# Expert weights loaded as rows of 8 KB per partition, gate and up accumulated over the full hidden width

## The chip, the core and the metric

The kernel runs on one core of one Trainium2 chip. Its engines are TensorE (PE, with PEld for the loading of the stationary operand), VectorE (DVE), ScalarE (ACT), GpSimd (POOL) and SyncE (SP); SP issues most of the DMAs, which 16 DMA engines carry out. The metric is the device time of one execution in microseconds.

## The reference, cut to what matters

One layer of a diffusion backbone over 512 latent tokens of width 1024. The part that the change touches is the last one, a mixture of 16 experts in which every expert picks its 64 best tokens:

```
D_MODEL = 1024; SEQ = 512; N_EXPERTS = 16; EC_CAPACITY = 2; D_EXPERT = 2048

def ec_moe(h, w_router, w_gate, w_up, w_down):
    b, l, d = h.shape
    cap = EC_CAPACITY * l // N_EXPERTS                      # 64 tokens for each expert
    aff = jax.nn.softmax((h @ w_router).astype(jnp.float32), axis=-1)
    gates, idx = lax.top_k(jnp.swapaxes(aff, 1, 2), cap)
    xs = jax.vmap(lambda hb, ib: hb[ib])(h, idx)
    hid = jax.nn.silu(jnp.einsum('becd,edf->becf', xs, w_gate)) * jnp.einsum('becd,edf->becf', xs, w_up)
    ys = jnp.einsum('becf,efd->becd', hid, w_down) * gates[..., None].astype(h.dtype)
    return jax.vmap(lambda yb, ib: jnp.zeros((l, d), yb.dtype).at[ib.reshape(-1)].add(yb.reshape(-1, d)))(ys, idx)
```

Ahead of it stand the adaLN modulation, a state-space branch, a differential attention and their merge; behind it a normalisation and the residual. All is float32. Each expert has three matrices of 8 MiB (gate and up 1024 x 2048, down 2048 x 1024), 24 MiB in all, 384 MiB for the 16 experts.

## The kernel before, in words

The program is written for one core with its order written out by hand: each engine runs its instructions in program order, and every load of an expert's weights is issued on SP in the order in which the code comes to it.

**Weight tiles.** `load_w` (L1579) takes the next free slot from the queue `E` and loads 1 MiB into it, 128 partitions x 2048 floats. A slot is one of the rotating buffers (tile name `we`), one of three pieces of a larger buffer (`wl`), or once each the buffers `gm` and `mo` before their later use. `done_w` puts the slot back in the queue behind the matmuls that read it. SP waits there until PE has released the slot, and then issues the next load. The load (L1592) takes two blocks of 128 rows, each 1024 floats (4 KB) wide: `"(k p) f -> p k f"`, so partition p gets row p and row 128 + p of the tile.

**One expert.** `hidden(e)` (L1629) works on half of the hidden width at a time (b = 0, 1). For each half it goes through four tiles of gate and then four of up, and accumulates both over the 1024 input channels in two PSUM tiles of tag `gu` (four buffers). A tile feeds two steps of 128 channels, each with two matmuls of 512 columns: the 64 tokens are the stationary operand, and the two matmuls write the lower and the upper 64 partitions of the accumulator. Each matmul shows as two records in the trace, so a tile is 8 records at L1643. Then ACT forms the Silu of gate into `sgm` (L1650), DVE multiplies by up (L1651), PE transposes the four blocks of 128 columns (L1654) into a PSUM tile `ht`, and DVE copies them to `hid` (L1655), from which `expert(e)` (L1657) takes the stationary operands of the down matmuls. Down has eight tiles of 256 rows (L1670), again two steps of 128 channels with two matmuls.

**Pairs.** Experts are gathered and scattered in pairs. After the hidden part of an odd expert, and ahead of its down, `gather` selects the tokens of the next pair with matmuls against a one-hot matrix (L1612), which DVE prepares (L1604). After an even expert `spread` (L1624) transposes the pair's gate-weighted one-hot matrix; after an odd one `scatter` adds the pair's output to the accumulators `facc` (L1684 to L1689). The first pair's gather is a generator, `first`, of which `hidden(0)` takes two steps ahead of each of its first tiles.

**The last expert.** After `hidden(15)` the down matrix is read in column blocks of 512, 256 and 256, with rows of 2 KB and 1 KB, in eight loads, and the closing normalisation of the first blocks runs between them. The output is stored at L1762.

**An earlier weight load with other rows.** The modulation weights (tile `araw`, L1099) are loaded as `w_ada[128 * (n % 8):128 * (n % 8) + 128, c0:c0 + 2048]`, 128 partitions with 8 KB each. The residual input (tile `x`, L1382) is loaded in eight parts of 32 partitions with 8 KB each.

Of the kernel before, what the change touches and what calls it, by code (L numbers as in the profile page):

```python
# [12 lines left out]
AF = mybir.ActivationFunctionType  # L13
OP = mybir.AluOpType
# [3 lines left out]
D = 1024  # L18
# [7 lines left out]
NE = 16  # L26
CAP = 64
FF = 2048
# [5 lines left out]
def layer(ctx: ExitStack, tc: tile.TileContext, A, out):  # L34
    nc = tc.nc
    PE, V, S, GP, DMA = nc.tensor, nc.vector, nc.scalar, nc.gpsimd, nc.sync
# [48 lines left out]
    def bank(name="b"):  # L85
        turn_[0] += 1
        if three[0] and turn_[0] % 3 == 0:
            return cbank(name)
        if three[0] is None:
            return pb.tile([128, 512], F32, name=name, tag="b")  # L90
        pair_[0] += 1
        return pb.tile([128, 512], F32, name=name, tag="bd"[pair_[0] % 2])
# [82 lines left out]
    ident = keep.tile([128, 128], F32, name="ident")  # L175
# [371 lines left out]
    for q in range(4):  # L547
        for par in range(2):
            PE.matmul(tl[64 * par:64 * par + 64, 64 * q:64 * q + 64], L[:, q], ident[0:64, 0:64],
                      start=True, stop=True, skip_group_check=True)  # L550
# [176 lines left out]
    for s in range(1, 96):  # L727
# [4 lines left out]
        sq = keep.tile([128, 2, 2, 16], F32, name="sq", bufs=2)  # L732
# [8 lines left out]
    def cobank(name):  # L741
# [8 lines left out]
                     op=OP.mult)  # L750
# [41 lines left out]
    wv = []  # L792
# [147 lines left out]
    for f in range(2):  # L940
        pgs = [bank2("glu")[:, 0:512] for _ in range(2)]
        for kt in range(4):
            for m in range(2):
                for n, (a, b) in enumerate(PASSES):
                    PE.matmul(pgs[m], wg[a][:, 512 * kt + 256 * f + 128 * m:512 * kt + 256 * f + 128 * m + 128], ygp[b][kt],
                              start=kt == 0 and n == 0, stop=kt == 3 and n == 2)
# [15 lines left out]
    for n in range(8):  # L962
        pq = bank("proj")
# [73 lines left out]
    for p in range(4):  # L1037
        t, w = kw.pop(0)
# [283 lines left out]
    pq = {}  # L1322
# [30 lines left out]
    for n in range(8, 16):  # L1353
        m = n % 8
# [33 lines left out]
    def psum(name, tag):  # L1388
        return ps_.tile([128, 512], F32, name=name, tag=tag, bufs=dict(s=2, gu=4, t=1, y=1)[tag])

    u_ = Carve(big("U2", "mo"))
    yp_, oh, sgm = u_(128, 2, D), u_(128, 4, 2, CAP), u_(128, 512)
# [175 lines left out]
    xst = [t[:, D:2 * D].rearrange("p (d e s) -> p d e s", d=8, e=2) for t in (gf_, gm_)]  # L1568
    hid = []
    wl = big("SR", "wl")  # L1570

    def strs(n):

        tags = [x for x in E if isinstance(x, str)][-n:]
        for x in tags:
            E.remove(x)
        return tags

    def load_w(src, r0, c0, cols=1024, n=1):  # L1579

        tag = E.popleft()
        if isinstance(tag, str):
            wv = regs.tile([128, 2048], F32, name="we", tag=tag)
        elif tag[0] == "SR":
            wv = wl[:, 2048 * tag[1]:2048 * tag[1] + 2048]
        else:
            wv = gm_ if tag[0] == "gm" else yp_.rearrange("p b d -> p (b d)")
        k = 2048 // cols
        wv = wv.rearrange("p (k f) -> p k f", k=k)
        for i in range(n):  # L1590
            a, b = k // n * i, k // n * (i + 1)
            DMA.dma_start(out=wv[:, a:b], in_=src[r0 + 128 * a:r0 + 128 * b, c0:c0 + cols].rearrange("(k p) f -> p k f", p=128))  # L1592
        return wv, tag

    def done_w(tag):
        if tag[0] not in ("U2", "gm"):
            E.append(tag)
# [8 lines left out]
    def gather(ep):  # L1606

        pick(ep, lambda i, n: r2[:, i:i + 1])
        for d in range(8):
            pg = psum("gat", "sst"[d % 3] if ep == 0 else "s")[:, 0:128]  # L1610
            for i in range(4):
                PE.matmul(pg, x1[i][:, 128 * d:128 * d + 128], oh[:, i].rearrange("p e s -> p (e s)"), start=i == 0, stop=i == 3)  # L1612
            o = xst[ep % 2][:, d].rearrange("p e s -> p (e s)")
            if d % 2:
                S.activation(o, pg, AF.Identity, scale=fs[:, 1, d:d + 1], bias=fs[:, 0, d:d + 1])
            else:
                V.tensor_scalar(o, pg, fs[:, 1, d:d + 1], fs[:, 0, d:d + 1], op0=OP.mult, op1=OP.add)
            yield
# [8 lines left out]
    wgt, wup, wdn = A["w_exp_gate"][0], A["w_exp_up"][0], A["w_exp_down"][0]  # L1627

    def hidden(e):  # L1629
        if not hid:  # L1630
            hid.append(None)
        for b in range(2):
            pgu = []
            for src in (wgt, wup):
                pq = psum("gu", "gu")
                for hk in range(4):
                    for _ in range(2):
                        next(first, None)
                    wv, tag = load_w(src[e], 256 * hk, 1024 * b)
                    for k in range(2):  # L1640
                        kt = 2 * hk + k
                        for j in range(2):
                            PE.matmul(pq[64 * j:64 * j + 64], xst[e // 2 % 2][:, kt, e % 2],  # L1643
                                      wv[:, k, 512 * j:512 * j + 512], start=kt == 0, stop=kt == 7, skip_group_check=True)
                    done_w(tag)
                pgu.append(pq)
            if hid[0] is None:
                t = regs.tile([128, 2048], F32, name="hid", tag=strs(1)[0])
                hid[0] = t.rearrange("p (b f i m) -> p b f i m", b=2, f=2, i=4)
            S.activation(sgm, pgu[0], AF.Silu)  # L1650
            V.tensor_tensor(sgm, sgm, pgu[1], op=OP.mult)  # L1651
            pt = psum("ht", "t")
            for i in range(4):
                PE.transpose(pt[:, 128 * i:128 * i + 128], sgm[:, 128 * i:128 * i + 128], ident)  # L1654
            V.tensor_copy(hid[0][:, e % 2, b].rearrange("p i m -> p (i m)"), pt)  # L1655

    def expert(e):  # L1657
        hidden(e)
        if e % 2:
            for _ in gather(e // 2 + 1):  # L1660
                pass
        hT_ = hid[0][:, e % 2]
        py = psum("yd", "y")
        for q in range(8):
            wv, tag = load_w(wdn[e], 256 * q, 0)
            b, jf = q // 4, (q % 4) // 2
            for k in range(2):
                i = 2 * (q % 2) + k
                for j in range(2):
                    PE.matmul(py[64 * j:64 * j + 64], hT_[:, b, i, 64 * jf:64 * jf + 64],  # L1670
                              wv[:, k, 512 * j:512 * j + 512], start=(q == 0 and k == 0), stop=(q == 7 and k == 1),
                              skip_group_check=True)
            done_w(tag)
        yp = yp_[:, (e // 2) % 2]
        P = slice(64 * (e % 2), 64 * (e % 2) + 64)
        S.activation(yp[P, 0:512], py[0:64], AF.Copy)  # L1676
        V.tensor_copy(yp[P, 512:1024], py[64:128])  # L1677
# [13 lines left out]
    first = gather(0)  # L1691
    next(first)
    for e in range(NE - 1):
        expert(e)
        if e % 2 == 0:
            spread(e // 2)
        if e % 2:
            if not facc:
                for x in strs(2):
                    t = regs.tile([128, 2048], F32, name="facc", tag=x)  # L1700
                    facc.extend((t[:, 0:D], t[:, D:2 * D]))
            for i in range(4):
                for j in range(2):
                    scatter(e // 2, i, slice(512 * j, 512 * j + 512))
# [3 lines left out]
    fin = [out_[i // 2][:, D * (i % 2):D * (i % 2) + D] for i in range(4)]  # L1708
    e, ep = NE - 1, NE // 2 - 1
    hidden(e)  # L1710

    root = keep.tile([128, 1], F32, name="root")
    S.activation(root, eps, AF.Sqrt)
    H = [slice(0, 512), slice(512, 768), slice(768, D)]
    sf = keep.tile([128, 3, 4], F32, name="sf")
    sq = hid[0].rearrange("p b f i m -> p (b f i m)")[:, 1024 * (1 - e % 2):1024 * (1 - e % 2) + 512]
    hT_ = hid[0][:, e % 2]

    def more(i, j):
        scatter(ep, i, H[j], "gu")  # L1720
# [4 lines left out]
    for j in range(3):  # L1725
        n = H[j].stop - H[j].start
        py = psum("yd", "yty"[j])[:, 0:n]
        nk = 2048 // n
        for q in range(16 // nk):
            wv, tag = load_w(wdn[e], 128 * nk * q, H[j].start, n, 1 + (q == 1 and j == 2))  # L1730
            for k in range(nk):
                kt = nk * q + k
                g = kt % 2
                PE.matmul(py[64 * g:64 * g + 64], hT_[:, kt // 8, kt % 4, 64 * (kt // 4 % 2):64 * (kt // 4 % 2) + 64], wv[:, k],
                          start=kt < 2, stop=kt > 13, skip_group_check=True)
            done_w(tag)
            if j == 1:
                more(2 * q, 0)
                more(2 * q + 1, 0)
        y = yp_[64:128, ep % 2, H[j]]  # L1740
        S.activation(y, py[0:64], AF.Copy)
        V.tensor_tensor(y, y, py[64:128], op=OP.add)
# [62 lines left out]
```

## Time and profile before

| what | value |
|---|---|
| median of 3 runs | 1625.45 us (1622.81 to 1628.09) |
| the profiled execution | 1623.83 us |
| its span, first to last instruction | 1622.1 us |
| busy PE, PEld, DVE, ACT, POOL | 86%, 45%, 35%, 17%, 11% of the span |
| mean granted TensorE clock | 0.951 |
| read from HBM | 461.65 MB |
| DMA packets | 148,132, of which 145,328 under 8 KB |

The profile is of one execution. Busy shares are means over the whole span, which has two very different parts: up to some 640 us the layer's first part, with many small steps on all engines, and behind it the experts. Matmul records overlap each other, so the busy time of PE is their union. A DMA share can stand a little over 1, since packets overlap on an engine.

### The profile page before, as it was taken

The page shows a single profiled execution, that of the slowest core. Times are in us where ns is not written, and L with a number is a line of the kernel's source. Part 1 is how long each engine was busy: PE and PEld are TensorE (multiplying, and loading weights), DVE is VectorE, ACT ScalarE, POOL GpSimd, SP SyncE. Part 2 cuts the span into 40 slices and gives each one's busy share as a digit, 9 for nine tenths or more (in the row PEclk, how much of TensorE's full clock was granted, in tenths as well). Part 3 has the DMA queues.
Part 4 walks back from the last instruction along what each step waited for, and adds up shares of the span by engine and source line. Part 5 has one row for each costly group of instructions (what it writes and reads, how often), then busy time and mean ns, then how long its engine had stood idle before and what let it go on. Part 6 is the DMA issues. An engine that isn't in the chain of part 4 may idle for free.

```text
span 1622.1 us, 18045 instructions
## 1 busy us (share of the span) xinstructions
PE 1397.1 (86%) x7228; PEld 735.9 (45%) x7228; DVE 563.6 (35%) x1378; ACT 283.1 (17%) x550; POOL 172.3 (11%) x113
## 2 busy tenths in 40 slices
PE   5989959997997894999989999879889879889874
PEld 3778746875664683334333343233233233233222
DVE  5799952286556647012021111111111111111103
ACT  3572104245432331000000000000000000000002
POOL 2123203453123300000000000000000000000003
PEclk9999979998997896999999999999999999999998
DMA  9212402222544168999999999999999999999994
GB/s 287 79 53 82 75 27 94 91 91 85 188 147 152 44 242 325 331 409 386 405 409 409 409 409 409 409 409 409 409 409 409 409 409 409 409 409 409 409 402 159
DMA packets 148132, 467.03 MB, mean 288 GB/s; under 512 B 16368, under 2 KB 36000, under 8 KB 145328
## 3 DMA queue, kind: packets, MB, share of 16 engines
q1 hardware_dynamic: 146880, 463.64, 74.8%
q10 hardware_dynamic: 816, 2.13, 0.5%
q8 instruction: 57, 0.93, 0.2%
q0 software_dynamic: 352, 0.11, 0.1%
q14 instruction: 27, 0.22, 0.0%
HBM read 461.65 MB, written 2.10 MB: 286 GB/s over the span
## 4 chain that ended last, share of the span: by engine, by line
PE 58%; DMA 20%; DVE 17%; ACT 3%; issue 2%; SPq 1%; POOL 0%; DVEq 0%; ACTq 0%
PE gu L1643 19%; DMA we<-in_w_exp_up_dram 10%; PE yd L1670 9%; DMA we<-in_w_exp_down_dram 6%; PE gat L1612 4%; PE sca L1684 4%; PE wo L1501 3%; PE gate L656 3%; PE u L528 2%; DVE SR L736 2%; DVE sp L733 1%; PE k L1034 1%; PE proj L656 1%; DVE sp L735 1%; DVE sq L734 1%
## 5 line engine op out<-in xcount | busy, mean ns | idle before, releaser
L1643 PE MATMUL gu<-we,gm 128*64 128x512 f32 x832 | 190.5, 604 | 15.2 <-DMA we<-in_w_exp_up_dram 11.2
L1643 PE MATMUL gu<-we,gf 128*64 128x512 f32 x816 | 188.7, 610 | 9.2 <-DMA we<-in_w_exp_up_dram 6.2
L1670 PE MATMUL yd<-we,hid 128*64 128x512 f32 x792 | 179.3, 597 | 11.7 <-DMA we<-in_w_exp_down_dram 11.7
L1651 DVE TENSOR_TENSOR mo<-mo,gu 128x512 f32<-128x512 f32 x32 | 22.0, 687 | 471.3 <-PE gu L1643 471.3
L1723 POOL TENSOR_TENSOR fin<-facc,gf 128x256 f32<-128x256 f32 (+1 forms) x12 | 10.6, 913 | 1030.7 <-DVE facc L1689 1030.7
L1643 PEld LDWEIGHTS gu<-we,gm 128*64 128x64 f32 x832 | 56.6, 138 | 139.2 <-issue 101.5
L1643 PEld LDWEIGHTS gu<-we,gf 128*64 128x64 f32 x816 | 56.6, 140 | 129.9 <-issue 103.4
L1670 PEld LDWEIGHTS yd<-we,hid 128*64 128x64 f32 x792 | 53.9, 137 | 124.9 <-issue 96.3
L656 PE MATMUL gate<-hh,wsp 128*128 128x512 f32 x384 | 97.6, 408 | 12.4 <-ACT sg L670 12.0
L1650 ACT ACTIVATE mo<-gu 128x512 f32<-128x512 f32 x32 | 19.1, 597 | 450.4 <-PE gu L1643 450.3
L1677 DVE COPY mo<-yd 64x512 f32<-64x512 f32 x15 | 10.4, 694 | 232.8 <-ACT mo L1676 232.8
L656 PEld LDWEIGHTS gate<-hh,wsp 128*128 128x128 f32 x384 | 73.0, 195 | 29.5 <-ACT sg L670 12.4
L1612 PE MATMUL gat<-mo,x 128*128 128x128 f32 x512 | 72.9, 307 | 9.6 <-DVE mo L1604 9.6
L1612 PEld LDWEIGHTS gat<-mo,x 128*128 128x128 f32 x512 | 68.8, 217 | 15.8 <-DVE mo L1604 10.3
L1684 PE MATMUL sca<-mo,gm 128*128 128x512 f32 (+1 forms) x136 | 61.6, 591 | 5.1 <-ACT mo L1676 5.1
L1676 ACT ACTIVATE mo<-yd 64x512 f32<-64x512 f32 x15 | 8.8, 589 | 284.3 <-PE yd L1670 284.3
L1501 PE MATMUL wo<-wo,mp 128*128 128x512 f32 x192 | 45.7, 394 | 2.1 <-DVE at L1360 2.1
L1643 PE MATMUL gu<-wl,gm 128*64 128x512 f32 x192 | 43.8, 596 | 3.7 <-DMA wl<-in_w_exp_up_dram 3.7
L1689 DVE TENSOR_TENSOR facc<-facc,sca 128x512 f32<-128x512 f32 (+1 forms) x60 | 38.6, 651 | 18.9 <-PE sca L1684 18.8
L1643 PE MATMUL gu<-wl,gf 128*64 128x512 f32 x192 | 44.5, 613 | 0.5 <-DMA wl<-in_w_exp_up_dram 0.5
L1654 PE MATMUL ht<-ident,mo 128*128 128x128 f32 x128 | 21.0, 287 | 27.5 <-DVE mo L1651 27.5
L1684 PEld LDWEIGHTS sca<-mo,gm 128*128 128x128 f32 x136 | 21.5, 188 | 44.7 <-DVE facc L1689 23.6
(427 smaller groups left out, 1872.8 us busy)
## 6 DMA issues: line engine op xcount, KB each, us to landing
we<-in_w_exp_gate_dram SPq DMA_DIRECT2D x124, 1024.0 KB, 18.4
we<-in_w_exp_down_dram SPq DMA_DIRECT2D x103, 1024.0 KB, 18.5
we<-in_w_exp_up_dram SPq DMA_DIRECT2D x82, 1024.0 KB, 18.8
wl<-in_w_exp_up_dram SPq DMA_DIRECT2D x44, 1024.0 KB, 18.9
wl<-in_w_exp_down_dram SPq DMA_DIRECT2D x24, 1024.0 KB, 18.9
araw<-in_w_ada_dram SPq DMA_DIRECT2D x16, 1024.0 KB, 6.2
wa<-in_w_ada_dram SPq DMA_DIRECT2D x16, 512.0 KB, 9.5
graw<-in_w_in_dram SPq DMA_DIRECT2D x4, 1024.0 KB, 5.5
```

The source lines that it names most:

```text
L528: PE.matmul(ps, tok(a, i, kt), w[b][:, kt % 2], start=kt == first and n == 0, stop=kt == last and n == 2)
L656: PE.matmul(ps, w[:, a, kt], x[b][kt], start=kt == 0 and n == 0, stop=kt == last and n == 2)
L736: V.tensor_tensor(h1, sp, sq, op=OP.add)
L1501: PE.matmul(po[j], mparts(a, kt)[:, 128 * i:128 * i + 128], wo[kt][:, D * b + 512 * j:D * b + 512 * j + 512].bitcast(F32R), start=kt == 0 ...
L1612: PE.matmul(pg, x1[i][:, 128 * d:128 * d + 128], oh[:, i].rearrange("p e s -> p (e s)"), start=i == 0, stop=i == 3)
L1643: PE.matmul(pq[64 * j:64 * j + 64], xst[e // 2 % 2][:, kt, e % 2], wv[:, k, 512 * j:512 * j + 512], start=kt == 0, stop=kt == 7, skip_grou ...
L1650: S.activation(sgm, pgu[0], AF.Silu)
L1651: V.tensor_tensor(sgm, sgm, pgu[1], op=OP.mult)
L1654: PE.transpose(pt[:, 128 * i:128 * i + 128], sgm[:, 128 * i:128 * i + 128], ident)
L1670: PE.matmul(py[64 * j:64 * j + 64], hT_[:, b, i, 64 * jf:64 * jf + 64], wv[:, k, 512 * j:512 * j + 512], start=(q == 0 and k == 0), stop=( ...
L1684: PE.matmul(po, gm[:, g0:g0 + 128], yp_[:, ep % 2, c], start=True, stop=True)
L1689: V.tensor_tensor(dst, dst, po, op=OP.add)
```

## The change

`load_w` gets a branch for tiles that take whole rows of their matrix: the tile is then a block of consecutive rows, each partition gets one row of gate or up (2048 floats) or two neighbouring rows of down (2 x 1024 floats), 8 KB in one piece. A tile of gate or up now holds 128 channels over the full width, so `hidden` accumulates both halves of the width side by side: eight tiles of gate into two accumulators, Silu of both into the half of `hid` that this expert does not fill (in place of `sgm`), eight tiles of up into two more accumulators, and then product, transposes and copy of the two halves, with PSUM tags `t` and `s`, the first copy on ACT and the second on DVE. As partition p of a down tile now holds rows 2p and 2p + 1, the transposes take every second column of a block of 256, except for the last expert, whose down is loaded as before. The first pair's gather takes one step per tile in place of two.

```
--- before.py
+++ after.py
@@ -1576,7 +1576,8 @@
             E.remove(x)
         return tags
 
-    def load_w(src, r0, c0, cols=1024, n=1):
+    def load_w(src, r0, c0, cols, n=1):
+
 
         tag = E.popleft()
         if isinstance(tag, str):
@@ -1586,6 +1587,9 @@
         else:
             wv = gm_ if tag[0] == "gm" else yp_.rearrange("p b d -> p (b d)")
         k = 2048 // cols
+        if not c0 and cols == src.shape[1]:
+            DMA.dma_start(out=wv, in_=src[r0:r0 + 128 * k].rearrange("(p k) f -> p (k f)", k=k))
+            return wv.rearrange("p (k f) -> p k f", k=k), tag
         wv = wv.rearrange("p (k f) -> p k f", k=k)
         for i in range(n):
             a, b = k // n * i, k // n * (i + 1)
@@ -1629,40 +1633,43 @@
     def hidden(e):
         if not hid:
             hid.append(None)
-        for b in range(2):
-            pgu = []
-            for src in (wgt, wup):
-                pq = psum("gu", "gu")
-                for hk in range(4):
-                    for _ in range(2):
-                        next(first, None)
-                    wv, tag = load_w(src[e], 256 * hk, 1024 * b)
-                    for k in range(2):
-                        kt = 2 * hk + k
-                        for j in range(2):
-                            PE.matmul(pq[64 * j:64 * j + 64], xst[e // 2 % 2][:, kt, e % 2],
-                                      wv[:, k, 512 * j:512 * j + 512], start=kt == 0, stop=kt == 7, skip_group_check=True)
-                    done_w(tag)
-                pgu.append(pq)
+        pgu = []
+        for src in (wgt, wup):
+            pq = [psum("gu", "gu") for _ in range(2)]
+            for kt in range(8):
+                next(first, None)
+                wv, tag = load_w(src[e], 128 * kt, 0, FF)
+                for b in range(2):
+                    for j in range(2):
+                        c = 1024 * b + 512 * j
+                        PE.matmul(pq[b][64 * j:64 * j + 64], xst[e // 2 % 2][:, kt, e % 2], wv[:, 0, c:c + 512],
+                                  start=kt == 0, stop=kt == 7, skip_group_check=True)
+                done_w(tag)
+            pgu.append(pq)
             if hid[0] is None:
                 t = regs.tile([128, 2048], F32, name="hid", tag=strs(1)[0])
-                hid[0] = t.rearrange("p (b f i m) -> p b f i m", b=2, f=2, i=4)
-            S.activation(sgm, pgu[0], AF.Silu)
-            V.tensor_tensor(sgm, sgm, pgu[1], op=OP.mult)
-            pt = psum("ht", "t")
+                hid[0] = t.rearrange("p (e b f) -> p e b f", e=2, b=2)
+            if src is wgt:
+                for b in range(2):
+                    S.activation(hid[0][:, 1 - e % 2, b], pq[b], AF.Silu)
+        for b in range(2):
+            act = hid[0][:, 1 - e % 2, b]
+            V.tensor_tensor(act, act, pgu[1][b], op=OP.mult)
+            pt = psum("ht", "ts"[b])
             for i in range(4):
-                PE.transpose(pt[:, 128 * i:128 * i + 128], sgm[:, 128 * i:128 * i + 128], ident)
-            V.tensor_copy(hid[0][:, e % 2, b].rearrange("p i m -> p (i m)"), pt)
+                c = slice(128 * i, 128 * i + 128) if e == NE - 1 else bass.ds(256 * (i // 2) + i % 2, 128, step=2)
+                PE.transpose(pt[:, 128 * i:128 * i + 128], act[:, c], ident)
+            (V.tensor_copy if b else S.copy)(hid[0][:, e % 2, b], pt)
 
     def expert(e):
         hidden(e)
         if e % 2:
             for _ in gather(e // 2 + 1):
                 pass
-        hT_ = hid[0][:, e % 2]
+        hT_ = hid[0][:, e % 2].rearrange("p b (i m) -> p b i m", i=4)
         py = psum("yd", "y")
         for q in range(8):
-            wv, tag = load_w(wdn[e], 256 * q, 0)
+            wv, tag = load_w(wdn[e], 256 * q, 0, D)
             b, jf = q // 4, (q % 4) // 2
             for k in range(2):
                 i = 2 * (q % 2) + k
@@ -1713,8 +1720,8 @@
     S.activation(root, eps, AF.Sqrt)
     H = [slice(0, 512), slice(512, 768), slice(768, D)]
     sf = keep.tile([128, 3, 4], F32, name="sf")
-    sq = hid[0].rearrange("p b f i m -> p (b f i m)")[:, 1024 * (1 - e % 2):1024 * (1 - e % 2) + 512]
-    hT_ = hid[0][:, e % 2]
+    sq = hid[0][:, 1 - e % 2, 0]
+    hT_ = hid[0][:, e % 2].rearrange("p b (i m) -> p b i m", i=4)
 
     def more(i, j):
         scatter(ep, i, H[j], "gu")
```

## Rows read from the trace of the kernel before

**Rows 1.** The page's 40 slices of the span: DMA busy tenths, GB/s

```profile
DMA  9212402222544168999999999999999999999994
GB/s 287 79 53 82 75 27 94 91 91 85 188 147 152 44 242 325 331 409 386 405 409 409 409 409 409 409 409 409 409 409 409 409 409 409 409 409 409 409 402 159
```

**Rows 2.** Windows: stretch, length, busy PE, PEld, DVE, ACT, POOL, PEclk, DMA share, GB/s

```profile
574.00:586.00 12.00, 12.00 (x64) 10.14 (x62) 5.29 (x17) 5.40 (x14) 0.00 (x0) 1.00 1.02 410
...
770.00:780.00 10.00, 9.56 (x46) 2.97 (x42) 0.32 (x1) 0.60 (x1) 0.00 (x0) 1.00 0.98 390
...
790.00:1570.00 780.00, 691.59 (x3110) 251.88 (x3108) 115.69 (x248) 35.64 (x65) 0.00 (x0) 0.98 1.02 409
```

**Rows 3.** Timeline of PE: start, length, instructions, idle time before and what ended it

```profile
1283.10 1.94 PE L1670 MATMUL yd<-we,hid 128*64 128x512 f32 x8 [0.62 <-DMA we<-in_w_exp_down_dram]
1285.66 1.94 PE L1670 MATMUL yd<-we,hid 128*64 128x512 f32 x8 [0.62 <-DMA we<-in_w_exp_down_dram]
```

**Rows 4.** Chain that ended last, in order of time: first scatter of four pairs

```profile
757.97 7.71 PE sca L1684 x16
...
870.85 7.70 PE sca L1684 x16
...
985.61 7.71 PE sca L1684 x16
...
1478.36 7.70 PE sca L1684 x16
```

**Rows 5.** Timeline of SP's queue: eight down loads, early and late

```profile
767.59 12.38 SPq L1592 DMA_DIRECT2D we<-in_w_exp_down_dram  x8
...
1249.39 20.37 SPq L1592 DMA_DIRECT2D we<-in_w_exp_down_dram  x8
```

**Rows 6.** DMA issues from 767 to 1557.9: count, KB each, us to landing

```profile
we<-in_w_exp_gate_dram SPq DMA_DIRECT2D x104, 1024.0 KB, 18.5
we<-in_w_exp_down_dram SPq DMA_DIRECT2D x86, 1024.0 KB, 18.5
we<-in_w_exp_up_dram SPq DMA_DIRECT2D x65, 1024.0 KB, 18.8
wl<-in_w_exp_up_dram SPq DMA_DIRECT2D x39, 1024.0 KB, 18.9
wl<-in_w_exp_down_dram SPq DMA_DIRECT2D x18, 1024.0 KB, 19.2
```

**Rows 7.** The page's DMA issues: the modulation weights

```profile
araw<-in_w_ada_dram SPq DMA_DIRECT2D x16, 1024.0 KB, 6.2
```

**Rows 8.** Windows in which araw, x and the last down are loaded

```profile
428.00:430.00 2.00, 2.00 (x9) 0.97 (x7) 1.12 (x4) 0.69 (x1) 0.00 (x0) 1.00 1.02 430
443.00:445.00 2.00, 2.00 (x11) 1.64 (x10) 0.00 (x0) 0.92 (x3) 0.00 (x0) 1.00 1.03 426
566.00:573.00 7.00, 7.00 (x34) 5.81 (x33) 1.08 (x4) 0.69 (x2) 0.00 (x0) 1.00 1.01 239
...
1577.00:1581.00 4.00, 3.39 (x16) 1.25 (x18) 1.13 (x2) 0.00 (x0) 0.00 (x0) 1.00 1.05 380
```

**Rows 9.** DMA packets from 443 to 445

```profile
DMA packets 120, 0.85 MB, mean 426 GB/s; under 512 B 16, under 2 KB 16, under 8 KB 16
```

**Rows 10.** The chain again: ends of the hidden halves of two experts

```profile
779.68 0.70 DVE mo L1651
780.42 0.66 PE ht L1654 x4
...
844.65 0.70 DVE mo L1651
...
847.28 9.00 PE gat L1612 x64
```

**Rows 11.** Timeline of PE at the last expert's change from up to down

```profile
1574.70 1.94 PE L1643 MATMUL gu<-we,gm 128*64 128x512 f32 x8 [0.61 <-DMA we<-in_w_exp_up_dram]
...
1582.93 1.94 PE L1734 MATMUL yd<-wl,hid 128*64 128x512 f32 x8 [0.86 <-DMA wl<-in_w_exp_down_dram]
```

## The prediction

> **What bounds the kernel now.** I read the slices of the page first. From slice 18 to the last but one the DMA engines are full and the rate stands at 409 GB/s, slice after slice [rows 1]: the second half of the span, in which the experts' weights are read, runs at the pace of one stream. The windows say the same of 780 us in one piece: 409 GB/s at a DMA share of 1.02, while PE is busy 691.59 of 780 us, 89% [rows 2]. That alone doesn't settle it, because PE is nearly as full. Two more views do. In PE's timeline late in the stretch, consecutive groups of 8 records (one tile of 1 MiB) start 2.56 us apart, each after a wait for a weight DMA, although the tile itself occupies PE 1.94 us [rows 3]. And 1.048576 MB / 409 GB/s = 2.564 us, so PE steps at the rate of the stream there.
>
> Then the chain, for how far PE is from being the bound itself. A pair of experts begins at its predecessor's scatter. The pair from 757.97 to 870.85 has no DMA step in its chain, so 112.88 us is what PE and its own waits need for 48 tiles; four later pairs take (1478.36 - 985.61) / 4 = 123.19 us, which is 48 x 2.566 us, the stream's pace [rows 4]. So PE has about 10 us of slack in each pair, and no more.
>
> Where does the stream begin to set the end? SP's queue shows it: the eight down loads of 767.59 are issued in 12.38 us, as fast as PE frees tiles; those of 1249.39 take 20.37 us, 2.55 us each [rows 5]. At 767.59 the stream had run dry, since PE released nothing while it scattered; the window 770 to 780 moves 390 GB/s, and from 790 there is no dip any more [rows 2]. Everything behind that point is the stream's. From there up to the last expert's down, 104 + 86 + 65 + 39 + 18 = 312 loads of 1 MiB are issued [rows 6], exactly 13 experts of 24. The eight loads of the last expert's down keep their short rows.
>
> **The change part by part.**
>
> *Rows of 8 KB.* The number of loads and their bytes stay (24 per expert); each has 128 rows of 8 KB in place of 256 of 4 KB. The stretch itself shows no 8 KB row, but an earlier one does: the loads of araw are 1 MiB on 128 partitions with 8 KB on each [rows 7], and the 2 us windows in which they alone run move 430 and 426 GB/s [rows 8]; the second of these holds 120 packets of which 104 have 8 KB or more [rows 9]. A second way to the same number: while rows of 2 KB and some shorter ones of the last down are moving, the rate is 380 GB/s [rows 8]. Per engine (16 of them) a 2 KB row then takes 2048 x 16 / 380 = 86.2 ns and a 4 KB row 4096 x 16 / 409 = 160.2 ns; 2 KB more cost 74.0 ns, so an 8 KB row should take 160.2 + 2 x 74.0 = 308.2 ns, which is 425 GB/s. Bounds: 409 (nothing gained in a long stream) and 430. I take 425, between the extrapolation and the window with the packet count: 2.467 us per tile, 0.097 less. Over 312 tiles that is 30.2 us (0 at 409; 0.1255 x 312 = 39.2 at 430).
>
> A rule speaks against it. The Trainium skill, DMA: Bandwidth & Descriptors, section Specifications, gives 512 bytes as the smallest transfer that reaches the line rate; by that, 4 KB rows lose nothing, the gain is 0 and the time 1624. The rows disagree: 380, 409 and 426 GB/s for growing rows, all above 512 bytes [rows 2, 8]. Its ceiling in the section Bandwidth, 435 GB/s, would be an estimate of 2.41 us a tile and a saving of 48 us; no window here reaches it.
>
> *Fewer, longer stalls in hidden.* Before, each half of the hidden width ends with a stall: product on DVE 0.70 from 779.68, transposes 0.66 from 780.42, so 1.40 us up to 781.08; the second half of an odd expert is followed by the gather, 844.65 to 847.28, 2.63 us [rows 10]. After, there is one stall per expert: product of half 0 (0.70), then that of half 1 (0.70) with the transposes of half 0 beside it, then the transposes of half 1 (0.66), some 2.1 us; the copy of half 0, now on ACT, lies beside these last transposes. Even experts gain 2.8 - 2.1 = 0.7, odd ones (with the gather's 1.23 behind) about 0.6. In the first pair, ahead of 767.59, where PE is the bound, this 1.3 us is on the path. Behind it, it only adds to PE's slack. The stepped columns in the transposes may make the weight load slower; no row shows it. Sixteen transposes a pair take 16 x 0.66 / 4 = 2.6 us; if each took three times as long, PE's pair would grow by 5.3 us, still inside the slack after the change (below). In the first pair this bound would cost 5.3 instead of gaining 1.3.
>
> *At nothing:* Silu of the gate runs beside the up matmuls, as before; four accumulators live at once in four buffers of that tag, and the next expert's gate comes behind their last readers; the other half of hid, which takes sgm's place, was last read by PE ahead of this expert. The gather steps of the first expert (one per tile in place of two per tile) are all past by the eighth tile both ways.
>
> *What comes late next.* The stream's pair becomes 48 x 2.467 = 118.4 us against PE's 112.88 - 1.3 = 111.6: 6.8 us of slack instead of 10. At 767.59 PE is 16 tiles behind the loads (384 - 312 - 8 = 64 are issued, a pair's 48 consumed), and that lead has to shrink before the stream is waited for; it shrinks by 2.7 tiles a pair, plus what the swing inside a pair gives, so PE first waits for weights about one pair later than now, and long before the end. The end of the kernel hangs on the stream as before: last up tile at 1574.70, the wait of 0.86 us ahead of 1582.93 in down [rows 11], which takes up the 0.7 us by which the last stall is longer.
>
> *Sum:* 30.2 + 1.3 = 31.5 us. The profiled execution took 1623.83, so 1592.3; the median of the runs is 1.6 above the profiled one, so 1594.
>
> **Rivals.**
>
> *PE becomes the bound.* For: PE's pair is only 5% shorter than the stream's new one. Against: the pair of 112.88 contains all waits there are [rows 4]. If the stepped transposes and the longer stall brought PE's pair to 120, the gain would be (123.2 - 120) x 6.5 pairs (790 to 1589) = 21 us: 1604.
>
> *The long stream doesn't follow.* The windows of 8 KB rows are bursts of two loads; a queue many loads deep might stay at 409. Against: 4 KB rows have the same rate in a burst of seven loads (574 to 586, 410 GB/s) and in the long stream [rows 2]. Then 0 to 1.3 us are gained: 1624.
>
> *Slower: long rows at a worse rate.* Loads of x with 8 KB rows (on 32 partitions) move only 239 GB/s at a full DMA share [rows 8]. Long rows can then be slow; if neighbouring rows read in one piece were of that kind, a tile would cost 4.39 us and the kernel 1625 + 1.82 x 312, about 2190. It decides at 409: every 1% below costs 8 us. Against: araw, on 128 partitions as here.
>
> **How the numbers follow.** The stream at 420 to 430 with PE keeping up: 0.74, 1585 to 1598. PE takes over in part: 0.10, 1598 to 1612. No change of rate: 0.10. Slower rows: 0.06. The range 1585 to 1610 holds the first and nearly all of the second. A difference under 0.3% (4.9 us) can't be told from none in this kernel; faster 0.84, the same 0.10, slower 0.06.
>
> **What would show it.** Right: GB/s of the slices near 425, steps of PE that wait for DMA of 2.47 us in place of 2.56, pairs of 118 us late in the stretch, 376 x 128 = 48,128 packets fewer, dry spell near 770 as long or longer. The first wait of PE for weights moves later. Wrong: a rate of 409 with these packets; a late chain without DMA steps and DMA share under 1 (PE the bound); transposes much over 0.66 us per four.

## The result, and the profile after

The change is faster: 1601.34 us median against 1624.86 (four runs of each, in turn on one chip), ratio 0.9853, 95% interval 0.9836 to 0.987. The profiled execution took 1600.69 us, its span 1598.9. The forecast was 1594: right in sign, 7 us too low, inside its range.

The page of the kernel after, in its 40 slices (DMA busy tenths and GB/s), and its packets:

```profile
DMA  9212402232354168799999999999999999999994
GB/s 280 90 54 83 76 27 96 82 102 86 133 203 144 29 237 342 269 420 420 392 420 419 420 420 419 420 420 420 419 420 420 419 420 419 420 420 419 419 408 154
DMA packets 100005, 467.03 MB, mean 292 GB/s; under 512 B 16369, under 2 KB 36001, under 8 KB 49073
```

The plateau stands at 420 where it stood at 409 [rows 1]; the same bytes now take 48,127 packets fewer. Behind the rise one slice stays below the plateau, 392, where there were two, 386 and 405. Windows of the kernel after show it more closely, and the first shows the gather ahead of the first pair's last down (the columns are those of [rows 2]: length, busy time of five engines, granted clock, DMA share, GB/s):

```profile
732.00:740.00 8.00, 7.98 (x66) 7.50 (x68) 2.85 (x10) 1.37 (x3) 0.00 (x0) 1.00 1.02 419
...
760.00:770.00 10.00, 10.00 (x42) 3.24 (x43) 2.32 (x4) 0.00 (x0) 0.00 (x0) 1.00 0.82 306
770.00:780.00 10.00, 10.00 (x50) 3.43 (x48) 0.00 (x0) 1.19 (x2) 0.00 (x0) 1.00 1.01 426
...
790.00:1500.00 710.00, 649.30 (x2936) 241.84 (x2936) 102.75 (x224) 40.03 (x73) 0.00 (x0) 0.98 1.01 420
```

From 790 on 420 GB/s without a dip: a tile of 1 MiB takes 1.048576 / 420 = 2.497 us, 0.067 less than the 2.564 of before [rows 2]. PE's timeline, late in the third pair and at the last expert, says the same (start, length, instructions, idle time before and what ended it):

```profile
941.10 1.94 PE L1645 MATMUL gu<-we,gf 128*64 128x512 f32 x8 [0.55 <-DMA we<-in_w_exp_up_dram]
943.60 1.94 PE L1645 MATMUL gu<-we,gf 128*64 128x512 f32 x8 [0.56 <-DMA we<-in_w_exp_up_dram]
...
1551.71 1.94 PE L1645 MATMUL gu<-we,gm 128*64 128x512 f32 x8 [0.59 <-DMA we<-in_w_exp_up_dram]
...
1559.95 1.94 PE L1741 MATMUL yd<-wl,hid 128*64 128x512 f32 x8 [0.87 <-DMA wl<-in_w_exp_down_dram]
```

Steps that wait for DMA are 2.50 us apart, 2.56 before [rows 3]. The last two lines answer to [rows 11]: the same wait ahead of the second group of down tiles, 0.87, and from the last up tile to the end of the span 1598.9 - 1551.7 = 47.2 us, 47.4 before. The tail has not moved.

The first scatter of the pairs in PE's timeline:

```profile
754.58 7.71 PE L1691 MATMUL sca<-mo,gm 128*128 128x512 f32 x16 [0.69 <-ACT mo L1683]
...
863.72 7.70 PE L1691 MATMUL sca<-mo,gm 128*128 128x512 f32 x16 [0.69 <-ACT mo L1683]
...
1098.69 7.70 PE L1691 MATMUL sca<-mo,gm 128*128 128x512 f32 x16 [0.69 <-ACT mo L1683]
...
1457.92 7.70 PE L1691 MATMUL sca<-mo,gm 128*128 128x512 f32 x16 [0.69 <-ACT mo L1683]
```

Three late pairs take (1457.92 - 1098.69) / 3 = 119.74 us, 48 tiles of 2.495; before it was 123.19 [rows 4]. The pair without a DMA step in its chain takes 109.14, 112.88 before.

To see where the first part of the gain lies, the chain of waits of both kernels in the first pair is laid side by side, from the first gather to the second. First the kernel before:

```profile
642.07 4.68 PE gat L1612 x24
...
683.05 13.91 PE yd L1670 x64
...
734.17 9.22 PE gat L1612 x64
```

and the kernel after:

```profile
641.95 3.75 PE gat L1616 x16
...
680.87 0.70 DVE hid L1657
...
681.61 0.75 PE ht L1661 x4
682.36 13.91 PE yd L1677 x64
...
732.02 7.99 PE gat L1616 x64
```

Counted from the first gather, so that what lies ahead of the experts plays no part, the first down begins after 40.98 us before and 40.41 after; the second gather after 92.10 and 90.07; the first scatter after 757.97 - 642.07 = 115.90 and 112.63. So 3.27 us are gained ahead of the point from which the stream sets the end: 0.57 in the even expert's hidden part, 1.46 in the odd one's, 1.23 in the gather. From the scatter to the end of the span it is 864.1 before and 844.3 after, 19.8 us less. Together 23.1. The change of the gather's time goes with its granted clock, of which more below.

SP's queue in its timeline, early and late, answers to [rows 5]:

```profile
764.20 12.34 SPq L1591 DMA_DIRECT2D we<-in_w_exp_down_dram  x8
...
1353.14 17.78 SPq L1591 DMA_DIRECT2D we<-in_w_exp_down_dram  x8
```

and what SP waits for, between 690 and 1560 us, most of it first (total, times, longest):

```profile
SPq L1591 <- DMA we<-in_w_exp_gate_dram: 175.2, 83, 3.3
SPq L1591 <- DMA we<-in_w_exp_down_dram: 165.2, 80, 2.2
SPq L1591 <- DMA we<-in_w_exp_up_dram: 159.1, 77, 2.4
SPq L1591 <- PE gu L1645: 62.8, 45, 13.3
```

The same view of the kernel before:

```profile
SPq L1592 <- PE gu L1643: 278.6, 146, 13.3
SPq L1592 <- PE yd L1670: 135.9, 76, 7.0
...
SPq L1592 <- DMA wl<-in_w_exp_up_dram: 7.7, 13, 0.6
```

SP is no longer held mainly by PE, from which it waits for a free tile, but by the landing of an earlier load.

### The profile page after: what moved, and what is told of

It is laid out like the page before. It is cut to its first block, busy times and chain, and to the rows that moved or that the text cites. A ratio compares the mean times of both kernels' runs of the same rounds, so it can differ in the third digit from the quotient of the medians.

```text
span 1598.9 us, 18037 instructions
## 1 busy us (share of the span) xinstructions
PE 1395.0 (87%) x7228; PEld 735.9 (46%) x7228; DVE 551.8 (35%) x1362; ACT 292.1 (18%) x566; POOL 172.6 (11%) x113
## 4 chain that ended last, share of the span: by engine, by line
PE 40%; DMA 39%; DVE 16%; ACT 2%; issue 2%; POOL 0%; DVEq 0%; ACTq 0%; SPq 0%
DMA we<-in_w_exp_up_dram 14%; DMA we<-in_w_exp_gate_dram 11%; DMA we<-in_w_exp_down_dram 11%; PE gu L1645 9%; PE yd L1677 5%; PE wo L1501 3%; PE gat L1616 3%; PE gate L656 3%; PE sca L1691 2%; DVE sp L733 2%; DVE SR L736 2%; PE u L528 2%; PE k L1034 1%; PE proj L656 1%; PE y L857 1%
## 5 line engine op out<-in xcount | busy, mean ns | idle before, releaser
L1657 DVE TENSOR_TENSOR hid<-hid,gu 128x512 f32<-128x512 f32 x32 | 21.9, 688 | 469.6 <-PE gu L1645 469.6
L1730 POOL TENSOR_TENSOR fin<-facc,gf 128x256 f32<-128x256 f32 (+1 forms) x12 | 10.6, 914 | 1010.7 <-DMA we<-in_w_exp_down_dram 1006.5
L1616 PE MATMUL gat<-mo,x 128*128 128x128 f32 x512 | 69.5, 295 | 10.2 <-DVE mo L1608 10.2
L1654 ACT ACTIVATE hid<-gu 128x512 f32<-128x512 f32 x32 | 19.0, 597 | 299.3 <-PE gu L1645 299.3
L1616 PEld LDWEIGHTS gat<-mo,x 128*128 128x128 f32 x512 | 64.4, 204 | 18.8 <-issue 15.2
L1662 ACT COPY hid<-ht 128x512 f32<-128x512 f32 x16 | 9.4, 587 | 257.2 <-PE ht L1661 257.2
L1501 PE MATMUL wo<-wo,mp 128*128 128x512 f32 x192 | 47.4, 404 | 2.3 <-DVE at L1360 2.3
L1696 DVE TENSOR_TENSOR facc<-facc,sca 128x512 f32<-128x512 f32 (+1 forms) x60 | 38.6, 650 | 18.8 <-PE sca L1691 18.8
## 6 DMA issues: line engine op xcount, KB each, us to landing
we<-in_w_exp_up_dram SPq DMA_DIRECT2D x106, 1024.0 KB, 19.9
we<-in_w_exp_down_dram SPq DMA_DIRECT2D x103, 1024.0 KB, 19.9
we<-in_w_exp_gate_dram SPq DMA_DIRECT2D x100, 1024.0 KB, 19.9
wl<-in_w_exp_gate_dram SPq DMA_DIRECT2D x27, 1024.0 KB, 19.9
wl<-in_w_exp_down_dram SPq DMA_DIRECT2D x24, 1024.0 KB, 19.9
wl<-in_w_exp_up_dram SPq DMA_DIRECT2D x21, 1024.0 KB, 19.9
```

Of the source, the lines that this page charges most:

```text
L1501: PE.matmul(po[j], mparts(a, kt)[:, 128 * i:128 * i + 128], wo[kt][:, D * b + 512 * j:D * b + 512 * j + 512].bitcast(F32R), start=kt == 0 ...
L1654: S.activation(hid[0][:, 1 - e % 2, b], pq[b], AF.Silu)
L1657: V.tensor_tensor(act, act, pgu[1][b], op=OP.mult)
L1696: V.tensor_tensor(dst, dst, po, op=OP.add)
```

## The experiments

Besides the rate of rows there were other explanations to tell apart: that the order of the accumulation brings a good part of the gain (B), that a long stream gives 8 KB rows less than a short burst for want of loads in flight (C), that neighbouring rows of down, read in one piece, are worse than whole rows of gate and up (D), that the other engines' traffic holds the stream down (E). Theory A is that the rate depends on the length of a row alone, with a fixed cost for each. Spans of several profiled executions differ by some 3 us in what lies ahead of the experts (in the change's second profile, below, the first gather comes 3.5 us later than above), so for each kernel the part behind the first gather is given too.

**Order alone, rows of 4 KB.** Gate and up accumulate over the full width as in the change, the loads stay short; down as before.

```
-            for kt in range(8):
...
-                wv, tag = load_w(src[e], 128 * kt, 0, FF)
+            for h in range(4):
                 for b in range(2):
...
+                    wv, tag = load_w(src[e], 256 * h, 1024 * b, 1024)
+                    for k in range(2):
+                        kt = 2 * h + k
```

> The changed order of work (gate and up accumulated over the full width, one stall per expert) with the old rows of 4 KB everywhere. Theory A, the rows are the gain: the stream stays at 409 GB/s and pairs at 123.2 us; only the 3.4 us by which the first pair's PE work ends earlier remain, so about 1621.5 us, ratio 0.998. Rival B, the order of work is the gain: about 1601 us as with the whole change, pairs near 120 us.

Measured: 1621.6 us, ratio 0.9988 (0.9978 to 0.9997). A window and PE's timeline of this kernel:

```profile
790.00:1500.00 710.00, 634.07 (x2846) 232.62 (x2847) 100.78 (x221) 39.40 (x72) 0.00 (x0) 0.98 1.02 409
```

```profile
754.56 7.71 PE L1689 MATMUL sca<-mo,gm 128*128 128x512 f32 x16 [0.69 <-ACT mo L1681]
```

The stream has the old rate and the first scatter the new time. From the first gather (642.20) to the end it is 976.5 us, 980.0 before: by the profiles the order is worth 3.5 us, all of it ahead of the stream's stretch; by the ratio of the runs it is 1.9 (0.5 to 3.6). B falls as the main cause, and holds for these few us.

**Long rows of down alone.** The order of before; only down takes the new loads and the stepped transposes.

```
+        if not c0 and cols == src.shape[1]:
+            DMA.dma_start(out=wv, in_=src[r0:r0 + 128 * k].rearrange("(p k) f -> p (k f)", k=k))
...
-                PE.transpose(pt[:, 128 * i:128 * i + 128], sgm[:, 128 * i:128 * i + 128], ident)
...
+                PE.transpose(pt[:, 128 * i:128 * i + 128], sgm[:, c], ident)
```

> The old order of work, with 8 KB rows for down alone (and the stepped columns that go with them), gate and up in 4 KB rows. Theory A, each load of 8 KB rows saves 2.564 - 2.497 = 0.067 us wherever it stands: 104 of the 312 loads behind the dry spell, 7.0 us less, about 1618 us, ratio 0.9957, and a stream of 412 to 413 GB/s. Rival B, the order of work is the gain: 1625 us. If long rows gain only when the whole stream has them (mixing of two row lengths on a ring costs something): between 1620 and 1625 us.

Measured: 1618.12 us, ratio 0.9963 (0.995 to 0.9977).

```profile
790.00:1500.00 710.00, 638.62 (x2876) 239.79 (x2874) 109.77 (x234) 31.77 (x59) 0.00 (x0) 0.98 1.02 412
```

From the first gather (642.23) to the end it is 974.1 us, 5.9 less than before. Its first scatter comes 0.65 later behind that gather than before: four stepped sets of transposes stand on the path, 0.75 us each in place of 0.66, and the first piece of the gather takes 4.97 in place of 4.68. So a third of the loads gives 5.9 + 0.65 = 6.5 us; all of them give 976.5 - 957.0 = 19.5, three times as much. The gain is the same per load for neighbouring rows of down as for whole rows of gate and up, which speaks against D.

**Streams by themselves.** The expert and modulation weights are loaded into rotating buffers, kind after kind.

```
    for i in range(32):
        load("r8d16", 16, rows(gate, i // 8, i % 8), (128, 2048))
    for i in range(32):
        load("r4d16", 16, cols(gate, 4 + i // 8, i % 8, 1024), (128, 2, 1024))
...
    for i in range(32):
        load("p8d16", 16, down[4 + i // 8][256 * (i % 8):256 * (i % 8) + 256].rearrange("(p k) f -> p (k f)", k=2), (128, 2048))
```

> Loads alone, no work on PE, ACT and POOL, one kind of load after the other, and zeros as output: all of the layer's arithmetic is left out. Kinds: rows of 8 KB of gate (16 buffers), 4 KB, 8 KB of the modulation weights (pitch 24 KB), 2 KB, 8 KB with 2 and with 4 buffers, pairs of rows of down, rows of 16 KB in loads of 2 MiB, 8 KB rows in loads of 2 MiB, and 8 KB rows issued in turn from SP and ACT. Theory A, a fixed cost per row on each engine of 2 x 160.2 - 312.1 = 8.3 ns: 4 KB 409, 8 KB 420 in all its kinds, 2 KB 388, 16 KB 426 GB/s. Rival C, the depth of the queue costs the rest: 8 KB with 2 or 4 buffers 424 to 426, with 16 buffers 420. Rival D, neighbouring rows cost the rest: modulation weights 426, gate and down 420. Rival E, the engines' own traffic costs it: 8 KB 425 or more in all kinds here.

Measured: 776.15 us in one run. Its windows, one for each kind (length, busy DVE and POOL, granted clock, DMA share, GB/s):

```profile
20.00:80.00 60.00, 0.00 (x0) 0.00 (x0) 1.00 1.01 422
100.00:160.00 60.00, 0.00 (x0) 0.00 (x0) 1.00 1.03 409
180.00:220.00 40.00, 0.00 (x0) 0.00 (x0) 1.00 1.01 421
235.00:280.00 45.00, 0.00 (x0) 0.00 (x0) 1.00 1.05 387
315.00:345.00 30.00, 0.00 (x0) 0.00 (x0) 1.00 1.00 406
395.00:440.00 45.00, 0.00 (x0) 0.00 (x0) 1.00 1.01 422
460.00:520.00 60.00, 0.00 (x0) 0.00 (x0) 1.00 1.01 422
635.00:650.00 15.00, 0.00 (x0) 0.00 (x0) 1.00 1.00 426
655.00:715.00 60.00, 0.00 (x0) 0.00 (x0) 1.00 1.01 422
720.00:755.00 35.00, 0.00 (x0) 0.00 (x0) 1.00 1.02 423
```

In order: whole rows of gate (8 KB) into 16 buffers; 4 KB rows; modulation weights, 8 KB of rows of 24 KB; 2 KB rows; 8 KB rows with only two buffers; with four; pairs of rows of down (8 KB); 16 KB rows in loads of 2 MiB; 8 KB rows in loads of 2 MiB; and what was left of 8 KB rows from SP and ACT in turn. Two kinds did not come about as meant. ACT issued its 16 loads from 496 to 578, as soon as it had buffers, beside the pairs of rows and the 16 KB rows; the last window holds SP's half alone, so the run says nothing of two issuing engines. And the window of 16 KB rows is short and not pure: by its 493 packets in 6.39 MB some seventh of its bytes are 8 KB rows of the next kind. Their rate is better taken from the 427 over 710 us of two kernels below, where one byte in eight still comes in 8 KB rows.

With the compute engines idle the rates are 409 and 422, nearly those of the kernels, 409 and 420: E falls, but for that last half per cent. Four buffers do as well as sixteen, only two cost something: C falls. Neighbouring rows give what whole rows do: D falls. Loads twice as large change nothing if the rows stay. What is left is the row, as in A: per engine (16 of them) a row takes 2048 x 16 / 387 = 84.7 ns, 160.2 for 4 KB, 310.6 for 8 KB and, at 427, 613.9 for 16 KB. That is about 9 ns for a row and 37.8 ns for each KB. Where these 9 ns are spent, at the reading or at the writing end, was not tried.

**The change once more**, unaltered, beside the next two on their chip.

> The changed kernel itself, unaltered, as the base for the two runs beside it: 1601 us, ratio 0.985 to 0.986, a stream of 420 GB/s.

Measured: 1602.75 us, ratio 0.9867 (0.9849 to 0.9884). From the first gather (645.42) to the end of the span (1601.7) it is 956.3 us, 957.0 in the first profile; the first scatter comes after 112.70 us, 112.63 there. The changed side of the 3.3 us of the first pair thus repeats. The kernel before was profiled once; the kernel with long rows of down alone, which has its order, took 116.55 to the first scatter.

**Rows of 16 KB.** Fourteen of sixteen MiB are loaded 2 MiB at a time, two rows of gate and up or four of down to a partition. The gather and the transposes take their columns in steps to match.

```
+    regsA = stackA.enter_context(tc.tile_pool(name="regsA", bufs=1))
...
+    stackA.close()
+    pool2 = ctx.enter_context(tc.tile_pool(name="late", bufs=1))
...
+            return pool2.tile([128, 4096], F32, name="wa2", tag=f"A{tag[1]}"), tag
...
+            DMA.dma_start(out=wv, in_=src[128 * r * p0:128 * r * (p0 + 1)].rearrange("(p r) f -> p (r f)", r=r))
...
-                PE.matmul(pg, x1[i][:, 128 * d:128 * d + 128], oh[:, i].rearrange("p e s -> p (e s)"), start=i == 0, stop=i == 3)
+                PE.matmul(pg, x1[i][:, bass.ds(256 * (d // 2) + d % 2, 128, step=2)], oh[:, i].rearrange("p e s -> p (e s)"), start=i == 0, stop=i == 3)
```

> The changed kernel with 14 of every 16 MiB of its weights in loads of 2 MiB with rows of 16 KB (two neighbouring rows of gate and up, four of down; the channels of the gathered tokens and of hid are stepped to match), the other two in loads of 1 MiB with rows of 8 KB, in the same 16 MiB of buffers. Theory A, a fixed cost per row: 426 GB/s for the long rows, 425.3 for the mix, 2.466 us per MiB in place of 2.497, so 312 x 0.031 = 9.7 us less than the change: 1591.5 us, ratio 0.980. Rival F, above 8 KB a row gains nothing in the long stream, or the coarser tiles starve the stream: 1600 us or more, ratio 0.985.

Measured: 1622.23 us, ratio 0.9993 (0.998 to 1.0005), a miss of 31 us. Two windows of this kernel:

```profile
600.00:640.00 40.00, 20.01 (x101) 16.35 (x100) 30.96 (x99) 7.24 (x19) 0.00 (x0) 0.68 0.00 1
...
790.00:1500.00 710.00, 644.22 (x2896) 250.65 (x2894) 101.41 (x222) 39.51 (x72) 0.00 (x0) 0.97 1.01 427
```

and of its chain the load that starts the experts:

```profile
640.78 8.29 DMA wa<-in_w_exp_gate_dram
```

The rate came as theory A has it, 427. But from 600 to 640, where the change loads at 342 GB/s, nothing is loaded: the wide buffers lie in one region that is given free as a whole, so the first load waits for its last earlier user, and SP issues nothing ahead of it. 342 GB/s over 40 us are 13.7 MB, worth 32.6 us at 420 GB/s. Neither A nor F had named this.

**Rows of 2 KB**, the other way, in the new order.

```
-                wv, tag = load_w(src[e], 128 * kt, 0, FF)
...
+                    ws = [load_w(src[e], 512 * h, 1024 * b + 512 * j, 512) for j in range(2)]
...
-            wv, tag = load_w(wdn[e], 256 * q, 0, D)
...
+            ws = [load_w(wdn[e], 512 * h, 512 * j, 512) for j in range(2)]
```

> The changed order of work with rows of 2 KB (blocks of 512 rows and 512 columns, two tiles used side by side), for the dose in the other direction. Theory A: 387 GB/s, 2.710 us per load in place of 2.564, 312 x 0.146 = 45.4 us more, less the 3.4 us of the shorter start: 1667 us, ratio 1.026. Rival G, PE and not the stream decides: 1622 us as with 4 KB rows, at a DMA share under 1.

Measured: 1672.03 us, ratio 1.0296 (1.0281 to 1.0311). Two of its windows:

```profile
760.00:770.00 10.00, 10.00 (x47) 3.36 (x48) 0.96 (x2) 0.00 (x0) 0.00 (x0) 1.00 1.04 386
...
790.00:1500.00 710.00, 605.15 (x2629) 233.15 (x2626) 91.61 (x207) 35.30 (x64) 0.00 (x0) 0.98 1.04 386
```

A tile takes 1.048576 / 386 = 2.717 us, 312 of them 47.7 more than at 409, or 44.2 with the order's 3.5 taken off. The other 4 us or so are probably of the same kind: this slower stream never runs dry after the first scatter (386 from 760 to 770, where the change falls to 306), so some 30 loads since 690 count too, by estimate 30 x 0.153 = 4.6 us.

**Rows of 16 KB with early loads.** The kernel of 16 KB rows, with a region for each pair of buffers in place of one for all.

```
+    for n, (st, tags) in enumerate(zip(stacks, PAIRS)):
+        p = st.enter_context(tc.tile_pool(name=f"pair{n}", bufs=1))
+        in_pair.update((x, p) for x in tags)
...
-    stackA.close()
+    for st in reversed(stacks):
+        st.close()
...
+    pool2 = [ctx.enter_context(tc.tile_pool(name=f"late{n}", bufs=1)) for n in range(7)]
```

> The long rows of e5 with each pair of buffers freed by its own earlier users, so that the loads again begin some 40 us ahead of the first expert's matmuls instead of behind 640 us. Theory A: the stream of e5, 427 GB/s, and the early loads of the change: 312 x (2.497 - 2.457) = 12 us less than the change's 1601 us, about 1590 us, ratio 0.978 to 0.980. Rival H, the coarser tiles of 2 MiB and the stepped columns of the gather cost in the first pairs what the rows give: 1600 us, ratio 0.985. Rival I, the loads are still late: 1610 to 1622 us and an empty slice near 600 us.

Measured: 1593.12 us, ratio 0.9815 (0.9794 to 0.9835). Three of its windows:

```profile
600.00:640.00 40.00, 21.26 (x107) 17.37 (x106) 30.63 (x102) 7.21 (x19) 0.00 (x0) 0.69 0.89 368
733.00:743.00 10.00, 9.84 (x66) 9.40 (x66) 2.99 (x11) 1.37 (x3) 0.00 (x0) 0.83 0.99 419
790.00:1500.00 710.00, 648.52 (x2958) 252.12 (x2954) 103.41 (x225) 39.98 (x73) 0.00 (x0) 0.98 1.01 427
```

The early loads are back, so the buffers were what the kernel of 16 KB rows had lost by: one region for all, with two wide buffers first in the queue. The order of the queue was changed along with the regions; the two were not tried apart. From the first gather (643.14) to the end of the span (1591.7) it is 948.6 us, 8.4 less than the change; the estimate from 427 against 420 is 312 x 0.041 = 12.8. Of the difference, 1.8 us lie in the first pair, whose gather takes 9.87 us at a granted clock of 0.83, where the change's takes 7.99 at 1.00; with stepped columns, as here, the other 16 KB kernel's takes 8.35 at 1.00. The other 2.6 were not traced; rates rounded to 1 GB/s leave some 2 us of them open. This kernel is the fastest of all.

## Why the prediction was right, and where its size was off

*That the stream sets the end from 767.59 on, over 312 loads* [rows 5, 6]: shown. The order alone, the long rows of one third, all long rows, rows of 2 KB and of 16 KB change the end by the rate of the stream in that stretch, with the order's 3.3 to 3.5 us ahead of it and, with 16 KB rows, 2.6 us open; the 2 KB rows need the loads ahead of it as well.

*Rows of 8 KB at 425 GB/s, 30.2 us*: this is the term that was mis-sized. The rate is 420 and the term 312 x 0.067 = 21.0 us by the rates, 19.5 to 19.8 by the spans (rates rounded to 1 GB/s leave 1 us or two open). Each of the two ways that led to 425 had a flaw. The windows of 430 and 426 [rows 8] are 2 us long; the same modulation weights in a window of 40 us of the streams give 421, while its windows of 2 us, one after the other from 164 to 206, give anything from 414 to 434. And the 380 GB/s of the extrapolation held shorter rows besides those of 2 KB, as the prediction said itself; pure 2 KB rows give 387. With that the same arithmetic would have been: 84.7 ns for 2 KB, 160.2 for 4 KB, so 160.2 + 2 x 75.5 = 311.2 ns for 8 KB, 421 GB/s, 2.491 us a tile, 22.8 us. The method was right and one number in it was not clean. The rate of 420 that came is the lower end of the prediction's main case, but its interval of time does not go with that end: at 420 its own sum gives 1625.45 - 21.0 - 1.3 = 1603, and not 1598. So the measured 1601 lies outside the interval of the case whose mechanism came (1585 to 1598) and inside that of PE taking over in part, whose mechanism did not come. That the whole range held the time is owed to this neighbour, and is in part luck.

*Fewer stalls in hidden, 1.3 us in the first pair*: it was 2.0, and the gather gave 1.23 more. The stall of an expert was put at some 2.1 us; in the chain after it is 0.70 + 0.75 = 1.45, since half 0's accumulators are complete ahead of the last up matmuls and its product, from 679.99, lies beside these, which end at 680.8. The gather's time was not thought of: it ran at a granted clock of 0.82 before, the mean of stretches at 1.2 and at 2.4 GHz, and runs at 1.00 (2.4 GHz throughout) after. Here are the windows around the two later gathers of the kernel before, against the 7.99 us at 1.00 above:

```profile
734.00:743.30 9.30, 9.13 (x64) 8.88 (x64) 3.09 (x11) 1.37 (x3) 0.00 (x0) 0.82 1.02 407
847.00:856.00 9.00, 8.72 (x63) 8.72 (x64) 3.20 (x11) 1.37 (x3) 0.00 (x0) 0.81 1.02 407
```

Ahead of the first of these PE stood idle twice, 0.86 and 1.23 us, around four transposes; after the change it stands once, 1.32 us. But the kernel of 16 KB rows with early loads has that one idle stretch too and a clock of 0.83 in this gather, so the idle time alone doesn't decide it. Nor does the order: the kernel of 2 KB rows, in the new order and behind 1.32 us each time, takes 9.62 us at 0.82 from 728.50 and 7.99 at 1.00 from 844.48, and the kernel before itself takes 8.08 at 1.00 from 1332.20, behind 1.23 us. So the 1.23 us are measured, but not shown to come from the change. Why the clock falls in some of these gathers stays open.

The two errors partly cancel: 10 us too much for the rows, 2 too little for the first pair, which is the miss of 8 in the gain.

*The stepped transposes*: dearer, as was left possible, and far from the bound of three times. The lines of the transposes, before and after (ns: lowest, median, highest):

```profile
L1654 PEld LDWEIGHTS ht<-ident,mo x128: 137/141/143, 667.0 to 1577.8; 128*128 128x128 f32 x128
```

```profile
L1661 PEld LDWEIGHTS ht<-ident,hid x128: 138/209/223, 680.7 to 1554.8; 128*128 128x128 f32 x128
```

With every second column the load of the stationary side takes 209 ns in place of 141; four transposes take 0.75 us, not 0.66.

*PE doesn't take over*: right. PE's pair went down to 109.14 us, further than the 111.6 forecast, and the stream's only to 119.74 instead of 118.4, so the slack is 10.6 us a pair and not 6.8. For the same reason the next step failed: *PE first waits for weights about one pair later*. It waits at 941.10, 15 us earlier than the kernel before:

```profile
956.59 1.94 PE L1643 MATMUL gu<-we,gf 128*64 128x512 f32 x8 [0.62 <-DMA we<-in_w_exp_up_dram]
```

Its lead shrinks by 10.6 us a pair, 10.3 before, where 6.8 was forecast. This costs nothing, as the stream is the bound either way.

*Dry spell as long or longer*: about the same. From 740 to 790 the windows miss 2.7 us of the old rate and 2.6 of the new.

*Tail, packets, down's last loads*: as forecast.

*The rivals*: PE as the bound, no change of rate, and slower rows are excluded by the 420 GB/s. The 239 GB/s that spoke for slower rows [rows 8] had shorter packets in its window too, 174 of 338; what 8 KB rows cost on 32 partitions alone was not tried. The rule of the Trainium skill (DMA: Bandwidth & Descriptors, section Specifications), by which rows above 512 bytes lose nothing, would have all these kernels equal; rows of 2, 4, 8 and 16 KB gave 387, 409, 422 and some 427 GB/s, and 2 KB rows in the kernel cost 3% (1.0296). The ceiling of 435 GB/s in the same section of the Trainium skill was not reached in any long stream here; 427 is the most.

## What to carry to other kernels

Where a stream of loads sets the end, each row costs a fixed time besides its bytes (here about 9 ns on each of 16 engines), so each doubling of the rows gains less: 22 GB/s, 13, 5. Take such a price from a long and pure window, not from 2 us or from a mixture: an error of 1% in the rate was 8 us here. And when buffers are laid out anew for longer rows, see first that the early loads stay early: one shared region cost some 29 us here (1622 against 1593), where 16 KB rows gave 8 over the change.

## What the runs showed of the hardware that was not expected

- The rate of an 8 KB row is the same, 421 to 422 GB/s, for whole rows, parts of 24 KB rows and neighbouring rows, for loads of 1 and 2 MiB, and for four buffers or sixteen; two buffers give 406.
- SP came to wait for the landing of earlier loads. The median of an up load from issue to landing is 19.9 us after, 18.8 before [rows 6]. Over the time of a tile, 2.497 and 2.564, that is 8.0 loads under way and 7.3. Whether the queue holds so many packets or so many loads was not tried; a stream with only four buffers has the rate of one with sixteen.
- The same gather of 64 matmuls takes 7.99 us at a granted clock of 1.00 and 9.62 at 0.82, both in the kernel of 2 KB rows, and the same stretch of idle time ahead of it (1.32 us) was followed by either.
- With every second column the load of a 128 x 128 stationary operand takes 209 ns in place of 141.
